# A two-layer attention trunk: gate paths ahead of the attention, values in six PSUM groups, an opening in units of 1, 2, 2, 2, 1 k-tiles

## The chip, the core and the metric

The kernel runs on one core of one Trainium2 chip. The metric is device time in microseconds (us) of one execution. The profiled execution is one of several; the trace belongs to it alone.

## What is computed

x has 256 tokens of 1024 features, c is one conditioning vector of 1024. There are two layers; each is a normalisation with shift and scale from c, an input projection, attention, a SiLU gate and an output projection. Everything is float32.

```python
for layer in range(DEPTH):
    ada = jnp.einsum('bd,de->be', c_act, w_ada[layer]) + b_ada[layer]
    shift, scale, gate = jnp.split(ada, 3, axis=-1)
    h = rms_norm(x, norm_g[layer]) * (1.0 + scale[:, None, :]) + shift[:, None, :]
    y = even_mixer(...) if layer % 2 == 0 else odd_mixer(...)
    x = x + gate[:, None, :] * y
return rms_norm(x, final_g)
```

The even mixer (layer 0) has two head groups. A: 8 heads of 64, one key and value head, window 128, a learned sink per head. B: 8 heads, 2 key and value heads, three branches (15 compressed blocks made by a small network, selected blocks, a window), added with sigmoid gates. The odd mixer (layer 1) has 16 heads of causal attention at this length. In both the attention's output is multiplied by silu(z), z a part of the input projection, and goes through the output projection.

## The kernel before

The program is not issued as it is written. `Plan.record` (L229) notes each instruction with what it depends on, and `Plan.issue` (L259) issues them all in the order of the table `ORDER` (L36 to L168). So the order on each engine is that of the table, and every instruction has line L256 in the profile; one goes by tiles. `plan.group` (L223) keeps matmuls together that use a part of TensorE's rows or columns at a time. For each tag a ring of buffers is taken in turn: five `raw` of 1 MB for weights that arrive (`RAW`), four `t4`, five `sm` and four `pT` for attention, and PSUM banks by tag (three pj, two s, one each of pt, o and m).

Every float32 product of a projection is three matmuls of halves: weights are cast to `whi` on ScalarE and the rest `wlo` is subtracted on VectorE (`split` L498), h likewise (hhi, hlo), and `mm3` (L533) adds hi x hi, hi x lo and lo x hi in PSUM.

**Opening.** c and x are read; x is transposed on TensorE into xT (part of bigA). The sums of squares of x give 1/rms, which is spread over the partitions by a matmul with `ones` and copied to `rb`. Then come eight k-tiles of 128 features. For each, 1 MB of w_ada (1024 rows, 128 columns each for shift and scale) arrives in runs of 512 bytes (`ada_tile` L401) and is summed with c as weights, by TensorE (`ada_rows` L419, 16 matmuls with 32-column weights in four column groups) or by VectorE (8 products of 256 columns into `acc`), as `ST_ON` says. `ada_shift_scale` (L450) makes the tile's shift and scale. `start_prep` (L688) then makes h from xT, rb, shift and scale with two products on VectorE and one activation, and loads the row of W_in: 128 features by 1688 columns, in four DMAs. `start_mm` (L712) adds the row's part for all 1688 columns, for two blocks of tokens, in PSUM: 24 matmuls. The w_ada of the next tile is loaded ahead of a tile's row, all in SP's queue.

**Layer 0.** After the opening come the remaining 256 columns of queries, rotation (`rope`), transposes, and the attention. `attn_pair` (L585) does one branch of two heads: four matmuls for the scores (a group), mask and minimum on VectorE, exponentials on ScalarE, four normalisations `sm<-sm,rc` on VectorE, six transposes, two copies, and four matmuls with the values into PSUM bank o (a group). B calls it twice a head pair (`b_pair` L938), A once (`a_pair` L924): 12 calls. `fin_o` (L790) copies the result to oT. The compressed branch is prepared by `compress` (L797) and `cmp_softmax` (L875); its keys `kcbd` and values `vz` are placed in blocks by two and eight small products onto memory that GpSimd had cleared. `cmp_pair` (L955) multiplies into a group of its own and adds it to oT on VectorE. `gated` (L970), four times, projects z (48 matmuls), takes tanh, and makes (1 + tanh) z and its product with oT on VectorE, then the two halves ghi and glo. Between these, `fill` places jobs: the sums with c for the gate of layer 0 and for shift and scale of layer 1. `out_proj` (L1025) follows.

**Layer 1** normalises and transposes x, then does four quads of heads (`attn_quad` L1115), each with its projections; after all of them come four `gated`, the output projection, the final norm and the output.

## Time and profile before

| | us |
|---|---|
| median of 3 runs | 318.71 |
| lowest, highest run | 318.41, 320.02 |
| the profiled execution's own time | 317.62 |
| its span in the trace | 315.8 |
| TensorE (PE) busy | 300.0 |
| VectorE (DVE) busy | 271.1 |
| ScalarE (ACT) busy | 189.9 |
| GpSimd (POOL) busy | 12.3 |

DMA moved 71.85 MB, 227 GB/s on the mean. How to read the lines: each group has the engine, the operation, out<-in with the program's tile names, the shapes, a count, then busy time, the mean ns of one and the idle time before them. A line of waits has the waiting engine and tile, the releaser, total us, count and longest. PEld is TensorE's weight load, which runs beside its matmuls. SP is the engine that issues most DMAs.

### The profile page before, as it was taken

How to read it: one execution, taken by the hardware profiler on the slowest of the kernel's cores; microseconds unless marked ns; L12 is line 12 of the kernel's file. 1: busy time of each engine (PE TensorE's matmuls, PEld its weight loads, DVE VectorE, ACT ScalarE, POOL GpSimd, SP SyncE). 2: the span in 40 equal slices, each digit the busy share in tenths (PEclk: the TensorE clock that was granted, in tenths of full speed). 3: DMA queues.
4: the chain of work that ended last, by engine and by line, in shares of the span. 5: the costliest groups of instructions: out<-in, count | busy, mean ns of one | idle time of the engine just before them, and what ended most of it. 6: DMA issues, size and time to landing. Idle time of an engine off the chain costs nothing.

```text
span 315.8 us, 6311 instructions
## 1 busy us (share of the span) xinstructions
PE 300.0 (95%) x2246; PEld 251.0 (79%) x2246; DVE 271.1 (86%) x744; ACT 189.9 (60%) x481; POOL 12.3 (4%) x30
## 2 busy tenths in 40 slices
PE   6788999999899999999999999999999999999991
PEld 6656787887677677898787689997899889988890
DVE  0289998999999999999998967787999998996873
ACT  3445435783758797797356675382965497654611
POOL 4200000000000000000010100000000000000021
PEclk9799999999999999999999999999999999999998
DMA  5999999999989954829699957646188644651003
GB/s 188 315 323 317 332 319 338 324 347 345 345 258 330 290 179 135 260 82 324 196 298 320 327 145 251 206 120 205 49 279 270 203 131 138 211 200 60 1 2 133
DMA packets 71280, 71.85 MB, mean 227 GB/s; under 512 B 3080, under 2 KB 62928, under 8 KB 71248
## 3 DMA queue, kind: packets, MB, share of 16 engines
q1 hardware_dynamic: 70528, 70.90, 72.0%
q10 hardware_dynamic: 592, 0.48, 0.5%
q8 instruction: 18, 0.29, 0.4%
q14 instruction: 14, 0.11, 0.1%
q0 software_dynamic: 128, 0.05, 0.1%
HBM read 70.38 MB, written 1.05 MB: 226 GB/s over the span
## 4 chain that ended last, share of the span: by engine, by line
PE 57%; DVE 22%; DMA 9%; ACT 4%; issue 4%; SPq 2%; POOL 1%; POOLq 0%; ACTq 0%; DVEq 0%
PE ps_pj L256 41%; DVE t L256 5%; DVE acc L256 5%; PE ps_pt L256 5%; PE ps_s L256 5%; PE ps_o L256 5%; DVE wlo L256 4%; DVE sm L256 4%; PE ps_m L256 2%; SPq L256 2%; DMA qT<-in_w_ada_dram 2%; DMA gate<-in_w_ada_dram 2%; DMA snk<-in_a_sinks_dram 2%; DMA raw<-in_w_in_even_dram 2%; DMA raw<-in_w_in_odd_dram 2%
## 5 line engine op out<-in xcount | busy, mean ns | idle before, releaser
L256 ACT CAST whi<-raw 128x512 fp32r<-128x512 f32 (+1 forms) x132 | 76.4, 600 | 47.4 <-PE ps_pj L256 28.9
L256 DVE TENSOR_TENSOR wlo<-raw,whi 128x512 fp32r<-128x512 f32 (+1 forms) x116 | 74.4, 659 | 5.4 <-ACT whi L256 5.3
L256 PE MATMUL ps_pj<-hhi,whi 128*128 128x256 f32 x256 | 73.0, 289 | 0.0
L256 PE MATMUL ps_pj<-hhi,wlo 128*128 128x256 f32 x256 | 72.2, 285 | 0.0
L256 PE MATMUL ps_pj<-hlo,whi 128*128 128x256 f32 x256 | 72.0, 283 | 0.0
L256 PEld LDWEIGHTS ps_pj<-hhi,whi 128*128 128x128 f32 x256 | 47.9, 188 | 1.4 <-issue 0.8
L256 PEld LDWEIGHTS ps_pj<-hlo,whi 128*128 128x128 f32 x256 | 48.1, 188 | 0.7 <-issue 0.3
L256 PEld LDWEIGHTS ps_pj<-hhi,wlo 128*128 128x128 f32 x256 | 47.9, 188 | 0.5 <-issue 0.2
L256 ACT ACTIVATE sm<-sm,mn 128x128 f32<-128x128 f32 (+1 forms) x76 | 34.1, 450 | 12.0 <-DVE mn L256 11.9
L256 DVE SCALAR_TENSOR_TENSOR acc<-raw,cz,acc 128x512 f32<-128x512 f32 x42 | 31.4, 746 | 0.5
L256 PE MATMUL ps_pj<-wlo,hhi 128*128 128x512 f32 (+2 forms) x72 | 27.3, 379 | 0.0
L256 PE MATMUL ps_pj<-whi,hhi 128*128 128x512 f32 (+2 forms) x72 | 26.3, 381 | 0.8 <-ACT hhi L256 0.7
L256 PE MATMUL ps_pj<-whi,glo 128*128 128x512 f32 (+1 forms) x72 | 26.7, 371 | 0.0
L256 PE MATMUL ps_pj<-wlo,ghi 128*128 128x512 f32 (+1 forms) x72 | 26.7, 371 | 0.0
L256 PE MATMUL ps_pj<-whi,ghi 128*128 128x512 f32 (+1 forms) x72 | 26.6, 374 | 0.0
L256 PE MATMUL ps_pj<-whi,hlo 128*128 128x512 f32 (+2 forms) x72 | 26.4, 368 | 0.0
L256 DVE SCALAR_TENSOR_TENSOR wlo<-raw,whi 128x512 fp32r<-128x512 f32 x32 | 21.0, 688 | 3.7 <-ACT whi L256 3.4
L256 DVE TENSOR_SCALAR sm<-sm,rc 128x256 f32<-128x256 f32 (+1 forms) x76 | 21.8, 318 | 0.3
L256 ACT COPY pT<-ps_pt 128x384 f32<-128x384 f32 x33 | 15.5, 471 | 10.2 <-PE ps_pt L256 9.5
L256 PE MATMUL ps_pt<-ta,sm 128*128 128x128 f32 x114 | 20.4, 280 | 0.0
L256 PEld LDWEIGHTS ps_pt<-ta,sm 128*128 128x128 f32 x114 | 13.0, 141 | 4.8 <-issue 2.9
L256 PEld LDWEIGHTS ps_pj<-whi,hhi 128*128 128x128 f32 x72 | 13.3, 188 | 3.6 <-ACT hhi L256 1.4
(206 smaller groups left out, 566.3 us busy)
## 6 DMA issues: line engine op xcount, KB each, us to landing
raw<-in_w_in_odd_dram SPq DMA_DIRECT2D x16, 1024.0 KB, 5.7
raw<-in_w_ada_dram SPq DMA_DIRECT2D x28, 512.0 KB, 5.6
qT<-in_w_ada_dram SPq DMA_DIRECT2D x24, 256.0 KB, 5.8
raw<-in_w_in_even_dram SPq DMA_DIRECT2D x5, 1024.0 KB, 7.2
raw<-in_w_in_even_dram SPq DMA_DIRECT2D x8, 576.0 KB, 5.5
raw<-in_w_out_even_dram SPq DMA_DIRECT2D x4, 1024.0 KB, 5.1
raw<-in_w_out_odd_dram SPq DMA_DIRECT2D x4, 1024.0 KB, 5.4
gate<-in_w_ada_dram SPq DMA_DIRECT2D x8, 256.0 KB, 6.1
```

The costliest lines, as they stand in the source:

```text
L256: self.ops.append(dict(key=eng.key, deps=deps, fn=lambda: getattr(real, name)(*args, **kw)))
```

## The change

Six things change together, and a new `ORDER` table puts them in another order.

1. *Opening.* `START` holds five units of 1, 2, 2, 2 and 1 k-tiles. A pair's w_ada is loaded at once, in runs of 1 KB (`start_ada`), into the rooms of qT and gate or into the four t4 in turn. The second number says how many of the eight row blocks VectorE sums (in 512 columns for a pair); TensorE takes the rest and adds VectorE's partial sums by a matmul with `ones` (`start_sums`), and a transpose puts the sums on the partitions. A row of W_in comes in two DMAs, with columns 256 to 640 in place of 0 to 256 and 512 to 640. x is multiplied by 1/rms ahead of its transposes, so hhi comes from xT in one activation.
2. *Gates first.* `gate_path` projects z and leaves (1 + tanh) z in oT. `gated` multiplies it by the attention's result straight from PSUM; `gated_parts` makes the halves. `fin_o`'s copies in layer 0 are gone. In layer 1 the gate path stands inside each quad.
3. *Values in six groups.* `attn_four` does two branches or two head pairs and returns the transposed weights; `attn_values` then multiplies all with the values, in one group and one PSUM bank. A has two groups of eight matmuls, B four of ten, with the compressed branch's two in front.
4. *Normalisation.* `ON_ACT` gives two of an `attn_four`'s eight normalisations, both of 256 columns, to ScalarE.
5. *Masks.* `blk` holds 0.5 in blocks and zero elsewhere: one product places the compressed keys, one the values.
6. *Order.* A goes first, then the compressed branch, then B.

The first place is SP's queue in the opening: names on the left are the rooms, w_ada and w_in_even the sources. Before:

```order
L256 DMA raw_101<-in_w_in_even_dram 128x152
L256 DMA qT_95<-in_w_ada_dram 128x4x128 x2
L256 DMA qT_96<-in_w_ada_dram 128x4x128 x2
L256 DMA raw_102<-in_w_in_even_dram 128x256
L256 DMA raw_102<-in_w_in_even_dram 128x1152
L256 DMA raw_102<-in_w_in_even_dram 128x128
L256 DMA raw_102<-in_w_in_even_dram 128x152
L256 DMA qT_97<-in_w_ada_dram 128x4x128 x2
L256 DMA gate<-in_w_ada_dram 128x4x128 x2
L256 DMA raw_103<-in_w_in_even_dram 128x256
```

And after, from the end of row 0 to row 3:

```order
L258 DMA raw_100<-in_w_in_even_dram 128x384
L258 DMA t_86<-in_w_ada_dram 128x2x256 x2
L258 DMA t_87<-in_w_ada_dram 128x2x256 x2
L258 DMA t_88<-in_w_ada_dram 128x2x256 x2
L258 DMA t_89<-in_w_ada_dram 128x2x256 x2
L258 DMA raw_101<-in_w_in_even_dram 128x1304
L258 DMA raw_101<-in_w_in_even_dram 128x384
L258 DMA qT_97<-in_w_ada_dram 128x2x256 x2
L258 DMA qT_98<-in_w_ada_dram 128x2x256 x2
L258 DMA qT_99<-in_w_ada_dram 128x2x256 x2
L258 DMA gate<-in_w_ada_dram 128x2x256 x2
L258 DMA raw_102<-in_w_in_even_dram 128x1304
```

One k-tile of w_ada (a pair of lines of x2) stood between rows before; now two k-tiles stand ahead of rows 1, 2 and 4, one ahead of row 6, and none between rows 2 and 3.

The second place is TensorE in B's head pairs; ps_o is the bank of the results, vb the values, pT the transposed weights, pcT and vz the compressed branch. Before:

```order
L256 MATMUL ps_o_93<-pT_140,vb 64x256
L256 MATMUL ps_o_93<-pT_141,vb 64x256
L256 MATMUL ps_o_93<-pT_140,vb 64x128
L256 MATMUL ps_o_93<-pT_141,vb 64x128
L256 MATMUL ps_pt_81<-ta,sm_132 128x128 x3
L256 MATMUL ps_pj_86<-hhi,whi_109 128x256
L256 MATMUL ps_pj_86<-hlo,whi_109 128x256
L256 MATMUL ps_pj_86<-hhi,wlo_113 128x256
```

And after, one whole group:

```order
L258 MATMUL ps_o_96<-pcT,vz 64x256 x2
L258 MATMUL ps_o_96<-pT_130,vb 64x256
L258 MATMUL ps_o_96<-pT_131,vb 64x256
L258 MATMUL ps_o_96<-pT_130,vb 64x128
L258 MATMUL ps_o_96<-pT_131,vb 64x128
L258 MATMUL ps_o_96<-bigA,vb 64x256 x2
L258 MATMUL ps_o_96<-bigA,vb 64x128 x2
```

The two branches and the compressed one, three groups with other work between them before, stand together.

```diff
-ST_ON = "ppvvpvvp"
-AHEAD = 1
+START = ((1, 0), (2, 4), (2, 6), (2, 6), (1, 4))
+GROUPED = 1
...
+ON_ACT = ((0, 1, 1), (1, 1, 1))
...
-            uses.append((a.tensor.name + "#", (p0, p1, 1), eng.key == "pe" and not accum))
+            uses.append((a.tensor.name + "#", (p0, p1, 1), eng.key == "pe" and (not accum or bool(kw.get("stop")))))
...
+                    if (n, i, t) in ON_ACT:
+                        A.mul(sms[i][:, a:b], sms[i][:, a:b], rc[:, n, i, t : t + 1])
+                    else:
+                        V.tensor_scalar(sms[i][:, a:b], sms[i][:, a:b], rc[:, n, i, t : t + 1], None, op0=ALU.mult)
...
+    def attn_values(po, jobs):
         ids = []
-        for t, (a, b) in enumerate(((0, P), (P, 3 * P))):
-            for i in range(2):
-                q, kT = qk[i]
-                ids.append(T.matmul(pSs[i][:, a:b], q(t), kT[:, 0 : b - a], start=True, stop=True))
+        for n, (cs, keys) in enumerate(jobs):
+            for m, (os, heads) in enumerate(keys):
+                for i in range(2):
+                    ids.append(T.matmul(
+                        po[64 * i : 64 * i + 64, cs + os.start : cs + os.stop],
+                        heads[i][0],
+                        heads[i][1],
+                        start=n == 0 and m == 0,
+                        stop=n == len(jobs) - 1 and m == len(keys) - 1,
+                        skip_group_check=True,
+                        tile_position=(0, 64 * i),
...
+        r = r0[:, t, :]
+        A.activation(t4(), xs[:, t, :], AF.Square, scale=D**-0.5, accum_out=r[:, 0:1])
+        G.tensor_scalar(r[:, 0:1], r[:, 0:1], EPS, None, op0=ALU.add)
+        G.tensor_tensor(r[:, 1:2], r[:, 0:1], ex0[:, 0:1], ALU.pow)
+        xn = t4()
+        V.tensor_scalar(xn[:, :512], xs[:, t, :512], r[:, 1:2], None, op0=ALU.mult)
+        A.mul(xn[:, 512:], xs[:, t, 512:], r[:, 1:2])
+        for hh in range(2):
+            px = bank("s" if t == 0 else "pj")
+            for j in range(4):
+                T.transpose(px[:, j * P : (j + 1) * P], xn[:, (4 * hh + j) * P : (4 * hh + j + 1) * P], ident)
+            (V.tensor_copy if hh == 0 else A.copy)(xT[:, 4 * hh : 4 * hh + 4, t * P : (t + 1) * P], px.rearrange("p (j s) -> p j s", j=4))
...
-        if ST_ON[g] == "v":
-            a = acc0[:, (g % 2) * 256 : (g % 2) * 256 + 256]
-            V.tensor_scalar(a, w[0][:, 0, :], cz[:, 0, 0:1], None, op0=ALU.mult)
-            for k in range(1, KT):
-                V.scalar_tensor_tensor(a, w[k // 4][:, k % 4, :], cz[:, k, 0:1], a, op0=ALU.mult, op1=ALU.add)
-            ada_shift_scale(0, g, 1, a=a, st=ones)
-        else:
-            ada_shift_scale(0, g, 1, a=ada_rows(w))
...
+        kk = 4 // n
+        w = []
+        for i in range(2 * n):
+            wt = room[i].rearrange("p (k s c) -> p k s c", k=kk, s=2)
+            for s in range(2):
+                Y.dma_start(wt[:, :, s, :], src[:, kk * i : kk * i + kk, s, P * g : P * (g + n)])
+            w += [wt[:, k] for k in range(kk)]
...
+    def start_sums(g, n, d, w):
+        a = sb([P, 512], "acc", 1)
+        av = a[:, : 256 * n].rearrange("p (s c) -> p s c", s=2)
+        for k in range(d):
+            if k == 0:
+                V.tensor_scalar(av, w[k], cz[:, k, 0:1], None, op0=ALU.mult)
+            else:
+                V.scalar_tensor_tensor(av, w[k], cz[:, k, 0:1], av, op0=ALU.mult, op1=ALU.add)
...
+            tq = [(cz[:, k, :], w[k][:, s_, cs]) for k in ks if k >= d]
+            if d and 0 in ks:
+                tq.append((ones[:, 0:32], av[:, s_, cs]))
...
+        T.transpose(pc[:, :P], asb[:, :P], ident)
...
-        Y.dma_start(raw[:, 1432:1688], W0[g * P : (g + 1) * P, 0:256])
-        Y.dma_start(raw[:, 0:1152], W0[g * P : (g + 1) * P, 1152:2304])
-        Y.dma_start(raw[:, 1152:1280], W0[g * P : (g + 1) * P, 512:640])
-        Y.dma_start(raw[:, 1280:1432], W0[g * P : (g + 1) * P, 2304:2456])
+        Y.dma_start(raw[:, 0:1304], W0[g * P : (g + 1) * P, 1152:2456])
+        Y.dma_start(raw[:, 1304:1688], W0[g * P : (g + 1) * P, 256:640])
+        return raw
+    def start_prep(g, raw):
         h = oT[:, 3 + g % 2, :]
-        V.scalar_tensor_tensor(h, xT[:, g, :], shs[:, 0, 1, g : g + 1], rb, op0=ALU.mult, op1=ALU.mult)
-        A.activation(hhi[:, g, :], h, AF.Identity, bias=shs[:, 0, 0, g : g + 1])
-        V.scalar_tensor_tensor(hlo[:, g, :], h, shs[:, 0, 0, g : g + 1], hhi[:, g, :].bitcast(F32), op0=ALU.add, op1=ALU.subtract)
+        sc, sh = shs[:, 0, 1, g : g + 1], shs[:, 0, 0, g : g + 1]
+        A.activation(hhi[:, g, :], xT[:, g, :], AF.Identity, bias=sh, scale=sc)
+        V.tensor_scalar(h, xT[:, g, :], sc, sh, op0=ALU.mult, op1=ALU.add)
+        V.tensor_tensor(hlo[:, g, :], h, hhi[:, g, :].bitcast(F32), ALU.subtract)
...
+    rooms = [spare[0:2], more, spare, more, spare[0:2]]
+    ahead, g = start_ada(0, START[0][0], rooms[0]), 0
+    for u, (n, d) in enumerate(START):
+        w, rows_w = ahead, [start_row(g)]
+        if u + 1 < len(START):
+            ahead = start_ada(g + n, START[u + 1][0], rooms[u + 1])
+        rows_w += [start_row(g + v) for v in range(1, n)]
+        start_sums(g, n, d, w)
+        preps = [start_prep(g + v, rows_w[v]) for v in range(n)]
+        for v in range(n):
+            start_mm(g + v, *preps[v])
+        g += n
...
-            V.tensor_scalar(kcbd[rs, :, 16 * i : 16 * i + 16], pk[rs, 0:32].rearrange("p (g b) -> p g b", g=2), 0.5, None, op0=ALU.mult)
+        V.tensor_tensor(
+            kcbd.rearrange("p g (i b) -> p g i b", i=2),
+            pk[:, 0:32].rearrange("p (g b) -> p g b", g=2).unsqueeze(2).to_broadcast([P, 2, 2, 16]),
+            blk[:, 4:6].unsqueeze(1).unsqueeze(3).to_broadcast([P, 2, 2, 16]),
...
-                V.tensor_scalar(vz[rs, g, j, :], pv[rs, 0:HD], 0.5, None, op0=ALU.mult)
+                T.matmul(pv[:, HD * g : HD * g + HD], hr[:, j, :, :].rearrange("p a b -> p (a b)"), w2["v"][:, j, :], start=(j == 0), stop=(j == 1))
+        V.tensor_tensor(
+            vz,
+            pv[:, : 2 * HD].rearrange("p (g d) -> p g d", g=2).unsqueeze(2).to_broadcast([P, 2, 4, HD]),
+            blk[:, 0:4].unsqueeze(1).unsqueeze(3).to_broadcast([P, 2, 4, HD]),
...
+        gated(po, 2 * u, 2, 0.5)
+        gated_parts(2 * u)
...
+        pts = attn_four([keys(0), keys(1)], maskc, None, [gv[:, 2 * hp_ : 2 * hp_ + 2, :, 1 + br] for br in range(2)])
         po = bank("o")
-        for br in range(2):
-            qk, vcl = [], []
-            for i in range(2):
-                rs = slice(64 * i, 64 * i + 64)
-                qk.append(
-                    (
-                        (lambda t, rs=rs: qbT[rs, hp_, t * P : (t + 1) * P]),
-                        kTb[rs, 2 * br + g, :],
-                    )
-                )
-                vcl.append(lambda b: vb[:, b, 3 * br + g, :])
-            attn_pair(qk, maskc, vcl, None, gv[:, 2 * hp_ : 2 * hp_ + 2, :, 1 + br], po, br == 0, br == 1)
-        fin_o(po, 4 + hp_)
-    def cmp_pair(hp_):
-        g = hp_ // 2
-        po = bank("o")
-        for i in range(2):
-            T.matmul(
-                po[64 * i : 64 * i + 64, :S],
-                vz[:, g, (2 * hp_ + i) % 4, :],
-                pcT[:, g, :],
-                start=True,
-                stop=True,
-                tile_position=(0, 64 * i),
-            )
-        V.tensor_tensor(oT[:, 4 + hp_, :], oT[:, 4 + hp_, :], po[:, :S], ALU.add)
-    def gated(w, zc, ft, coef, tag="pj"):
+        attn_values(po, ([(0, cmp_keys(hp_))] if cmp else []) + [(0, keys_of(lambda b, br=br: vb[:, b, 3 * br + g, :], pts[br])) for br in range(2)])
+        gated(po, 4 + hp_, 1, 0.25)
+        if hp_ % 2:
+            gated_parts(3 + hp_)
...
-        V.tensor_tensor(oT[:, 4 + hp_, :], oT[:, 4 + hp_, :], po[:, :S], ALU.add)
...
+    def gate_path(w, zc, ft, tag="pj"):
         pz = proj_F(w, zc, tag)
-        tt = t4()
-        th, og = tt[:, :512], tt[:, 512:].rearrange("p (j s) -> p j s", j=2)
+        th = oT[:, ft : ft + 2, :].rearrange("p j s -> p (j s)")
         A.activation(th, pz, AF.Tanh, scale=0.5)
         V.scalar_tensor_tensor(th, th, 1.0, pz, op0=ALU.add, op1=ALU.mult)
-        V.scalar_tensor_tensor(
-            og.rearrange("p j s -> p (j s)"),
-            oT[:, ft : ft + 2, :].rearrange("p j s -> p (j s)"),
-            coef,
-            th,
-            op0=ALU.mult,
-            op1=ALU.mult,
-        )
-        A.copy(ghi[:, ft : ft + 2, :], og)
-        V.tensor_tensor(glo[:, ft : ft + 2, :], og, ghi[:, ft : ft + 2, :].bitcast(F32), ALU.subtract)
+    def gated(po, ft, n, coef):
+        V.scalar_tensor_tensor(oT[:, ft : ft + n, :], po[:, : n * S].rearrange("p (a s) -> p a s", s=S), coef, oT[:, ft : ft + n, :], op0=ALU.mult, op1=ALU.mult)
+    def gated_parts(ft):
+        A.copy(ghi[:, ft : ft + 2, :], oT[:, ft : ft + 2, :])
+        V.tensor_tensor(glo[:, ft : ft + 2, :], oT[:, ft : ft + 2, :], ghi[:, ft : ft + 2, :].bitcast(F32), ALU.subtract)
...
-        A.copy(oT[:, 2 * u : 2 * u + 2, :], po.rearrange("p (a s) -> p a s", a=2))
+        gated(po, 2 * u, 2, 0.5)
+        gated_parts(2 * u)
+    jobs += ada_jobs(ada_gate, 1, G1_ON, 2)
...
+        gate_path(W1, 3 * D + 256 * u, 2 * u, "p1")
         attn_quad(u, qk)
```

More of the change, by code (lines that the diff above doesn't have):

```diff
@@ L342, in tile_trunk @@
     G.memset(ex0, -0.5)
+    blk = const([P, 6], "blk")
+    G.memset(blk, 0.0)
+    for j in range(6):
+        rs = slice(32 * j, 32 * j + 32) if j < 4 else slice(64 * j - 256, 64 * j - 192)
+        G.memset(blk[rs, j : j + 1], 0.5)
     cz = const([P, KT, 32], "cz")
@@ L647, in tile_trunk, with keys_of @@
+    def keys_of(vcols, pts):
+        return [
+            (os, [(vcols(b), pts[i][:, ks]) for i in range(2)])
+            for b, (ks, os) in enumerate(((slice(0, S), slice(0, S)), (slice(S, 3 * P), slice(P, S))))
+        ]
     bigA = const([P, 2304], "bigA")
@@ new lines, in tile_trunk, with a_quad, keys @@
+    pj_banks, s_banks = ring["ps_pj"][0], ring["ps_s"][0]
+    ring["ps_pj"] = [pj_banks[0:3], 0]
+    m_banks = ring["ps_m"][0]
+    ring["ps_s"] = [s_banks + pj_banks[3:3], 0]
+    def a_quad(u):
+        def keys(i):
+            rs = slice(64 * i, 64 * i + 64)
+            return lambda n, t: (qaT[rs, 2 * u + n, t * P : (t + 1) * P], kTb[rs, 4, : P * (t + 1)])
+        sk = [[[snk[:, o + 4 * u + 2 * n + i : o + 4 * u + 2 * n + i + 1] for i in range(2)] for n in range(2)] for o in (8, 0)]
+        pts = attn_four([keys(0), keys(1)], maska, sk, None)
+        po = bank("o")
+        attn_values(po, [(n * S, keys_of(lambda b: vb[:, b, 2, :], pts[n])) for n in range(2)])
+        gated(po, 2 * u, 2, 0.5)
+        gated_parts(2 * u)
```

325 lines of the change are left out of this document (159 added, 166 removed), and 262 rows, old and new, of the table ORDER.

## The prediction

> **What bounds the kernel now.** I read the page's first two parts, then a table of stages, then the waits of the weight loads between 62 and 180 us, the chain between 108 and 135 us and the costliest groups of VectorE.
>
> The page gives the span, the busy shares, and the slices of 7.9 us.
>
> ```profile
> span 315.8 us, 6311 instructions
> PE 300.0 (95%) x2246; PEld 251.0 (79%) x2246; DVE 271.1 (86%) x744; ACT 189.9 (60%) x481; POOL 12.3 (4%) x30
> ...
> PE   6788999999899999999999999999999999999991
> ...
> DVE  0289998999999999999998967787999998996873
> ```
>
> The stage table has the stretch, then busy time of PE, PEld, DVE, ACT and POOL, the granted clock, the DMA share and GB/s.
>
> ```profile
> 0.00:18.00 18.00, 13.04 (x87) 10.82 (x88) 3.24 (x14) 8.56 (x18) 5.09 (x18) 0.91 0.91 259
> 18.00:62.00 44.00, 42.20 (x235) 32.93 (x236) 40.17 (x96) 20.73 (x47) 0.00 (x0) 1.00 1.09 325
> 62.00:112.00 50.00, 48.13 (x430) 37.13 (x429) 49.30 (x187) 35.41 (x110) 1.58 (x3) 1.00 1.00 321
> 112.00:150.00 38.00, 37.95 (x315) 31.36 (x314) 37.62 (x123) 31.24 (x95) 0.00 (x0) 1.00 0.57 191
> 180.00:250.00 70.00, 70.00 (x563) 64.84 (x566) 59.57 (x142) 42.84 (x99) 0.00 (x0) 1.00 0.63 196
> 260.00:303.00 43.00, 43.00 (x291) 37.44 (x290) 36.81 (x67) 25.87 (x52) 0.90 (x2) 1.00 0.35 115
> ```
>
> Three regimes stand there. Until 62 us the DMA engines are full (share 1.09, 325 GB/s). In layer 0's attention, 62 to 150 us, TensorE and VectorE are both nearly full: VectorE is busy 49.30 + 37.62 = 86.92 of 88 us. In layer 1 TensorE alone is full, and VectorE has about 15% free. But a busy PE is not a PE at its peak: its weight loads still wait for semaphores in the middle stage.
>
> ```profile
> PEld ps_m L256 <- DVE vz L256: 1.1, 2, 0.7
> PEld ps_pt L256 <- ACT sm L256: 1.0, 2, 0.6
> ...
> PEld ps_m L256 <- DVE h L256: 0.2, 1, 0.2
> ```
>
> These are the first two and the last of 21 rows (total us, count, longest) that name another engine; together they hold 10.2 us. So at most some 10 us of layer 0 can be won by relieving other engines, and the rest only by giving TensorE less to do.
>
> **Part 1, the opening (0 to 62 us).** The last row's cast waits for its load until 55.84, and the opening's last matmul starts at 63.47, the next work at 63.66.
>
> ```profile
> 11.96 0.27 PE L256 MATMUL ps_pt<-ta,crow 8*128 8x8 f32 x1
> ...
> 12.95 1.07 PE L256 MATMUL ps_m<-qT,cz 128*32 128x256 f32 x16
> ...
> 17.88 0.74 PE L256 MATMUL ps_pj<-whi,hhi 128*128 128x512 f32 x2
> ...
> 55.84 0.62 ACT L256 CAST whi<-raw 128x512 fp32r<-128x512 f32 x1 [0.34 <-DMA raw<-in_w_in_even_dram]
> ...
> 63.47 0.35 PE L256 MATMUL ps_o<-whi,hlo 128*128 128x408 f32 x1
> 63.66 0.60 PE L256 MATMUL ps_pt<-ta,bigA 128*128 128x128 f32 x4
> ```
>
> The first main matmul (17.88) should come earlier: c is no longer transposed behind x (11.96), and the broadcast of 1/rms is gone. I put it at 15.2, a guess on which nothing hangs: any start up to 17.5 gives the same end, since row 1 lands when it did. Bytes in queue order: x 1.05 MB, w_ada 1.05 MB per k-tile, a row of W_in 0.86 MB. Before, the queue holds x, two k-tiles of w_ada, row 0, one k-tile and row 1: 5.92 MB. After, it holds x, one k-tile, row 0, a pair and row 1: the same 5.92 MB. By 18 us 259 x 18 = 4.66 MB had moved; with the rate of 20 to 30 us (329 GB/s, quoted below) row 1 lands at 18 + 1.26/0.329 = 21.8, and with 1.2 us for its cast and subtraction, twice the cast's 0.62, tile 1 starts at 23.0. Row 2 is different: a whole pair stands before it, so 8.88 MB are needed against 7.83 before, and it lands at 30.8, 3.2 us later than before. Tile 2 starts at 32.0. A tile takes (45.8 - 1.8)/8 = 5.5 us (17.88 to 63.66, less TensorE's idle 44 - 42.20), so TensorE waits 32.0 - 28.5 = 3.5 us there. Row 4 also stands one k-tile further back, at 12.70 MB: it is ready at 43.6, where tile 4 would be due at 43.0. Four tiles from there end at 65.6: **+1.9 us**. The other rows have the byte counts that they had.
>
> Bounds: for the better, the end is held by the bytes, 1.05 for x, 8 x 1.05 of w_ada and 8 x 0.86 of rows, some 16.35 MB altogether.
>
> ```profile
> 20.00:30.00 10.00, 9.72 (x46) 7.54 (x47) 9.64 (x25) 3.11 (x7) 0.00 (x0) 1.00 1.11 329
> ...
> 70.00:80.00 10.00, 9.86 (x106) 7.65 (x109) 9.70 (x43) 4.32 (x16) 1.58 (x3) 1.00 1.09 343
> ```
>
> The first stretch moves w_ada in runs of 512 bytes beside the rows, the second has only longer ones: 329 against 343 GB/s. After the change pairs come in 1 KB runs; at the second rate the bytes take 47.7 us instead of 49.7, a gain of 2.0 as the bound. The Trainium skill ("DMA: Bandwidth & Descriptors", Specifications) puts the line-rate limit at 512 bytes or more; by that rule the longer runs bring nothing, this bound would be 0 instead of -2.0, and the sum would stand. The trace agrees nearly: the difference is 4%. For the worse, the pair's tiles t4 are also the room in which x is squared and scaled, so SP's queue waits there with rows 1 to 7 behind it; another 3.5 us, the size of the wait before tile 2, gives +5.4. VectorE's share in the opening falls (16 products with shift and scale at 0.48 become 16 simpler ones; sums in 512 columns):
>
> ```profile
> L256 DVE SCALAR_TENSOR_TENSOR acc<-qT,cz,acc 128x256 f32<-128x256 f32 x20 | 9.7, 484 | 0.6
> ...
> L256 DVE SCALAR_TENSOR_TENSOR hlo<-oT,shs,hhi 128x256 fp32r<-128x256 f32 x7 | 3.4, 482 | 0.1
> ```
>
> This is worth a few us on VectorE, but bytes lead there, so I take 0.
>
> **Part 2, layer 0's attention and gates.** What VectorE does there:
>
> ```profile
> L256 DVE TENSOR_SCALAR sm<-sm,rc 128x256 f32<-128x256 f32 x24 | 8.4, 360 | 0.1
> L256 DVE SCALAR_TENSOR_TENSOR t<-oT,t 128x512 f32<-128x512 f32 x4 | 2.7, 686 | 0.1
> L256 DVE SCALAR_TENSOR_TENSOR t<-t,ps_pj 128x512 f32<-128x512 f32 x4 | 2.7, 682 | 0.1
> L256 DVE TENSOR_SCALAR vz<-ps_m 32x64 f32<-32x64 f32 x8 | 1.8, 220 | 0.1
> L256 DVE TENSOR_TENSOR oT<-oT,ps_o 128x256 f32<-128x256 f32 x4 | 1.7, 414 | 0.0
> ...
> L256 DVE TENSOR_TENSOR gate<-ps_m,gate 128x512 f32<-128x512 f32 x1 | 0.7, 684 | 0.0
> ```
>
> - Twelve of the 24 normalisations go to ScalarE: -12 x 0.360 = -4.3.
> - Four additions of the compressed branch go, since it shares the PSUM group: -4 x 0.414 = -1.7.
> - Eight small products for the compressed values become one of 512 columns: -8 x 0.220 + 0.684 = -1.1; two for the keys become one: -0.2.
> - The product with the gate reads PSUM, four times 128x512 (4 x 0.686 = 2.7) before, then twice 128x512 and four times 128x256 (2 x 0.682 + 4 x 0.484 = 3.3): +0.6.
>
> Sum on VectorE: -6.7 us out of a stage where 1.1 us is free. The products out of PSUM are a place where a rule speaks against the change. One-input products show it in the trace:
>
> ```profile
> L256 DVE TENSOR_SCALAR t<-ps_s,shs 128x128 f32<-128x128 f32 x8 | 3.0, 403 | 0.0
> ...
> L256 DVE TENSOR_SCALAR sm<-sm,rc 128x128 f32<-128x128 f32 x24 | 6.6, 281 | 0.0
> ```
>
> From PSUM 403 ns, from SBUF 281. The two-input products that `gated` uses cost the same either way (682 with PSUM, 686 without), so I charge nothing. The Trainium skill ("VectorE: DVE Perf Modes", Why PSUM operands drop a tier) says that a PSUM operand holds fp32 at the slowest rate; by that rule, read for every product and with the row's 0.122 us for each 128 columns, two products of 512 columns and four of 256 would cost 16 x 0.122 = 2.0 more, and the sum would be that much higher. The trace agrees for one input, not for two.
>
> TensorE sheds group changes. The chain names the groups (each fp32 matmul is recorded as two passes):
>
> ```profile
> 115.43 1.45 PE ps_o L256 x16
> ...
> 124.37 0.58 PE ps_o L256 x4
> ...
> 130.31 0.80 PE ps_o L256 x8
> ```
>
> Before: eight groups for B's two branches and four for A at 0.80, and four compressed ones at 0.58: 12 x 0.80 + 4 x 0.58 = 11.9. After: two groups of eight matmuls (x16) at 1.45, four of ten at 1.45 + 0.58, less 0.15 for the change that is saved (2 x 0.80 - 1.45): 2.9 + 7.5 = 10.4. So -1.5 on TensorE.
>
> ScalarE takes the twelve normalisations and loses the copies out of PSUM:
>
> ```profile
> L256 ACT COPY oT<-ps_o 128x256 f32<-128x256 f32 x9 | 3.3, 370 | 1.2 <-PE ps_o L256 1.0
> ...
> L256 ACT ACTIVATE t<-t 128x256 f32<-128x256 f32 x1 | 0.4, 417 | 0.3 <-DVE t L256 0.3
> ```
>
> 12 x 0.417 - 8 x 0.370 = +2.0, in a stage where it has 88 - 66.65 = 21 us free; if that cover fails, 2.0 is the price. The bounds for the stage: TensorE's -1.5 alone, if nothing else waits less, to -1.5 less most of the 10.2 us of waits: -10. I take **-5.5**, nearer VectorE's 6.7, because it is the fuller engine; the 1.2 us between are what I leave to waits that the new order brings.
>
> A new wait: values start only when all branches of a head pair are done and, for B, when the compressed branch is there. On PE the projections of the gates are queued round it, and they cover it.
>
> **Part 3, layer 1 and the tail.** Gates move between the quads and four copies go from ScalarE. TensorE is busy 70.00 of 70.00 and 43.00 of 43.00 us with the same matmuls: **0**, from -1.5 (the group changes' size again) to +1.5.
>
> The profiled execution's own time is 317.62 (its span of 315.8 and 1.8 around it). The sum against it: 317.6 + 1.9 - 5.5 = 314.0. It is 1.1 us below the median of the three runs, 318.71, so the median comes out at **315.1**.
>
> **The rivals.**
> - *Both gains come whole* (faster). Row 2's wait is hidden by work already loaded, the longer runs bring 2.0, and layer 0 loses 9: 317.6 - 2.0 - 9 + 1.1 = 307.7. For it: VectorE is full for 88 us. Against: TensorE's idle in 112:150 is only 0.05. Chance 0.17.
> - *TensorE becomes the bound at once* (no change). VectorE's 6.7 is slack nobody needs; only -1.5 stays and the opening eats it: 317.6 + 1.9 - 1.5 + 1.1 = 319.1. For it: PE busy 48.13 of 50 and 37.95 of 38. Against: the 10.2 us of waits. It is also what would be seen if the regrouping did not do what it says. Chance 0.15.
> - *Paired loads starve TensorE* (slower). SP holds at the t4 rooms and rows 2 and 4 stand behind one k-tile more: +5.4, with only -1.5 behind it: 317.6 + 5.4 - 1.5 + 1.1 = 322.6. It decides from the point where the opening's last matmul lies later than 63.7 + 5.5, about 69. For it: 325 GB/s is all the queue gives. Against: only two of eight rows stand later in the order of bytes. Chance 0.13.
>
> **How the numbers follow.** The forecast keeps 0.55, with a range of its own of 311.5 to 318.5. A measurement of this kernel can tell about 0.5%, 1.6 us: faster is below 317.1, slower above 320.3. Faster: most of 0.55, say 0.49, and 0.17, together 0.66. Same: 0.15 and 0.06 of the forecast, 0.21. Slower: 0.13. The range of 8 in 10 reaches to the price of the fast rival and short of that of the slow one: 307.5 to 321.5.
>
> **What would show it.** Tile 1's first main matmul near 23, tile 2's after a wait for row 2 near 32, before tile 4 hardly one, the last of the opening near 65.6; VectorE's busy time in the attention stage some 6.7 lower; fewer waits of PEld; layer 1 as long as before. The forecast is wrong if the opening's end moves by over 3 us, if layer 0's attention is shorter by under 3 or over 8 us, or if layer 1's length changes by over 2.

## The result and the profile after

The changed kernel takes 307.85 us (median of 4 runs, 306.97 to 309.57), the one before 319.26 (4 runs): a ratio of 0.965, 95% interval 0.9595 to 0.9704. The forecast was 315.1 with a range of 307.5 to 321.5 and a gain of 1.1%; the gain is 3.5%, three times that.

The page of the changed kernel, its span, its busy shares, and the slices, which are 7.6 us long now:

```profile
span 304.9 us, 6320 instructions
PE 290.6 (95%) x2292; PEld 247.9 (81%) x2292; DVE 262.8 (86%) x709; ACT 189.6 (62%) x484; POOL 12.0 (4%) x35
...
PE   7688999999999999999999999999999999999991
...
DVE  0679988899999999999989968998779898996973
```

The same stretches as in the prediction's table of stages:

```profile
0.00:18.00 18.00, 13.70 (x94) 11.36 (x94) 7.81 (x24) 9.01 (x17) 5.09 (x23) 1.00 0.91 308
18.00:62.00 44.00, 41.77 (x306) 34.23 (x306) 38.32 (x82) 25.64 (x65) 0.00 (x0) 1.00 1.07 370
62.00:112.00 50.00, 49.56 (x467) 41.61 (x466) 49.58 (x187) 40.21 (x126) 1.54 (x3) 1.00 0.85 273
112.00:150.00 38.00, 38.00 (x298) 30.33 (x296) 37.42 (x113) 27.49 (x76) 0.00 (x0) 1.00 0.79 247
```

The line to stop at is the second. The DMA engines are as full as before (1.07 against 1.09), yet they move 370 GB/s in place of 325. In the attention TensorE's idle time is down to 0.4 us, and VectorE is as full as it was (49.58 + 37.42 of 88).

Three places in TensorE's timeline cut the span into stages that both kernels have: the start of the first main matmul, of the opening's last one into ps_s, and of the last one of layer 0's output projection. The changed kernel:

```profile
14.18 0.73 PE L258 MATMUL ps_pj<-whi,hhi 128*128 128x512 f32 x2 [1.55 <-ACT hhi L258]
...
60.56 0.40 PE L258 MATMUL ps_s<-whi,hlo 128*128 128x512 f32 x1
...
162.76 0.40 PE L258 MATMUL ps_s<-whi,glo 128*128 128x512 f32 x1
```

And the kernel before, with 17.88 quoted in the prediction. The opening's work into ps_s runs on behind the row at 63.47 that the prediction took for its last:

```profile
65.02 0.39 PE L256 MATMUL ps_s<-whi,hlo 128*128 128x512 f32 x1
...
172.67 0.40 PE L256 MATMUL ps_pj<-whi,glo 128*128 128x512 f32 x1
```

| stage, us | before | after | change | forecast |
|---|---|---|---|---|
| to the first main matmul | 17.9 | 14.2 | -3.7 | -2.7 |
| opening, first to last | 47.1 | 46.4 | -0.8 | +4.6 |
| the two together | 65.0 | 60.6 | -4.5 | +1.9 |
| layer 0 after it | 107.6 | 102.2 | -5.4 | -5.5 |
| layer 1 and tail | 143.1 | 142.1 | -1.0 | 0 |

Layer 0 is right to 0.1 us. What failed is the opening, by 6.4 us. There ScalarE's casts wait for the rows as follows:

```profile
20.62 0.62 ACT L258 CAST whi<-raw 128x512 fp32r<-128x512 f32 x1 [0.18 <-DMA raw<-in_w_in_even_dram]
...
28.83 1.14 ACT L258 CAST whi<-raw 128x512 fp32r<-128x512 f32 x2 [5.23 <-DMA raw<-in_w_in_even_dram]
...
39.11 1.66 ACT L258 CAST whi<-raw 128x512 fp32r<-128x512 f32 x3 [5.21 <-DMA raw<-in_w_in_even_dram]
```

These are rows 1, 2 and 4. The prediction had them land at 21.8, 30.8 and 42.4 (the last is its 43.6 less the 1.2 us for cast and subtraction): each cast starts earlier than that, row 4's by 3.3 us.

The second trace of the changed kernel, taken later on another occasion, starts its main matmuls at 15.85 and ends the opening at 63.06, 2.0 us earlier than before in place of 4.5; its layer 0 is 102.3 long. So the opening's gain differs between executions, and the stages of one trace are read beside the medians. Eight traces below leave the changed opening as it is (these two and six whose edits lie in layer 0): they start it at 13.9 to 15.9 and end it at 60.5 to 63.1, which is 2.0 to 4.6 us before 65.02. The kernel before moves as well: a version of it that is the same up to its third k-tile (b_lean below) starts at 18.9.

### The profile page after: what moved, and what is told of

Read it like the earlier page. It is cut to its first block, busy times and chain, and to the rows that moved or that the text cites. A ratio compares the mean times of both kernels' runs of the same rounds, so it can differ in the third digit from the quotient of the medians.

```text
span 304.9 us, 6320 instructions
## 1 busy us (share of the span) xinstructions
PE 290.6 (95%) x2292; PEld 247.9 (81%) x2292; DVE 262.8 (86%) x709; ACT 189.6 (62%) x484; POOL 12.0 (4%) x35
## 3 DMA queue, kind: packets, MB, share of 16 engines
HBM read 70.38 MB, written 1.05 MB: 234 GB/s over the span
## 4 chain that ended last, share of the span: by engine, by line
PE 85%; DMA 5%; DVE 3%; POOL 2%; issue 2%; ACT 1%; POOLq 0%; ACTq 0%; DVEq 0%; SPq 0%
PE ps_pj L258 53%; PE ps_s L258 11%; PE ps_pt L258 8%; PE ps_o L258 7%; PE ps_m L258 6%; DMA qT<-in_w_ada_dram 2%; DMA t<-in_w_ada_dram 2%; DVE acc L258 1%; DMA ta<-in_tbl_a_dram 1%; DVE t L258 1%; POOL parts L258 1%; POOL r L258 1%; ACT t L258 1%; DVE xs L258 0%; DVE wlo L258 0%
## 5 line engine op out<-in xcount | busy, mean ns | idle before, releaser
L258 PE MATMUL ps_pj<-hhi,whi 128*128 128x256 f32 x256 | 72.2, 287 | 0.0
L258 PE MATMUL ps_pj<-hhi,wlo 128*128 128x256 f32 x256 | 71.0, 285 | 0.0
L258 ACT ACTIVATE sm<-sm,mn 128x128 f32<-128x128 f32 (+1 forms) x58 | 26.0, 450 | 13.1 <-DVE mn L258 13.1
L258 PE MATMUL ps_pj<-whi,ghi 128*128 128x512 f32 (+1 forms) x56 | 20.6, 369 | 0.0
L258 PE MATMUL ps_pj<-whi,glo 128*128 128x512 f32 (+1 forms) x56 | 20.5, 366 | 0.0
L258 PE MATMUL ps_pj<-wlo,ghi 128*128 128x512 f32 (+1 forms) x56 | 20.5, 369 | 0.0
L258 PE MATMUL ps_pt<-ta,sm 128*128 128x128 f32 x87 | 16.9, 279 | 0.0
L258 ACT COPY pT<-ps_pt 128x384 f32<-128x384 f32 x25 | 11.9, 474 | 6.4 <-PE ps_pt L258 6.2
L258 PEld LDWEIGHTS ps_pj<-whi,hlo 128*128 128x128 f32 x72 | 13.6, 189 | 1.9 <-issue 0.2
L258 PEld LDWEIGHTS ps_pj<-wlo,hhi 128*128 128x128 f32 x72 | 13.5, 188 | 1.9 <-DVE wlo L258 0.2
```

What stands on the lines that cost most here:

```text
L258: self.ops.append(dict(key=eng.key, deps=deps, fn=lambda: getattr(real, name)(*args, **kw)))
```

## The experiments

Theory R says that the opening gained by the longer runs of its loads. Theory S says that it gained by its earlier start. For layer 0, theory V has VectorE as the limit and theory P has TensorE with its changes between groups. All times are medians; the ratio is to the kernel before on the same chip, and a difference such as +1.9 us is to 307.85. The changed kernel itself, measured again on another chip, took 309.28 (ratio 0.9663). So a difference of under some 2 us between medians tells little by itself, and the length of the stage in the trace is given with it: layer 0 takes 102.2 to 102.7 us in six traces whose edits, if any, lie in the opening; with more work on VectorE there (a_vopen) it takes 103.3.

**Runs of 512 bytes.** The paired k-tiles' w_ada in runs of 512 bytes again, same bytes, same count of loads:

```diff
-                Y.dma_start(wt[:, :, s, :], src[:, kk * i : kk * i + kk, s, P * g : P * (g + n)])
...
+                else:
+                    m = 2 * i + s
+                    k4, sv, v = 4 * (m // 4), (m % 4) // 2, m % 2
+                    Y.dma_start(
+                        wt[:, s].rearrange("p s c -> p (s c)").rearrange("p (q c) -> p q c", q=4),
+                        src[:, k4 : k4 + 4, sv, P * (g + v) : P * (g + v + 1)],
+                    )
```

This version also lets an instruction be issued behind its place in `ORDER` where its inputs come later; in the trace the opening's loads are issued in the same order and number as in the changed kernel.

> The changed kernel, with the w_ada of the paired k-tiles read again in runs of 512 bytes, by as many loads of the same size (each load takes four row blocks of 128 columns; they land in other places of the tiles, so shift and scale of six k-tiles are computed from the wrong numbers). Theory R, the run length: the opening gained because longer runs move w_ada faster (370 GB/s between 18 and 62 us against 325 before). 6.3 MB at 325 in place of some 400 GB/s take 3 to 6 us longer, ahead of rows 1 to 7, so the total rises by 3 to 6 us, to 311 to 314, and the rate of 18 to 62 us falls to 335 or less. Theory S, the earlier start: the opening gained because its first main matmul came 3.7 us earlier and the steps of a tile got shorter, and the rate is a symptom; the total stays within 1 us of 307.9.

Measured: 312.25, ratio 0.9806 (0.9753 to 0.9859), 4.4 us above 307.85. The table of stages, for 18 to 62 us:

```profile
18.00:62.00 44.00, 39.64 (x275) 32.53 (x276) 33.41 (x73) 21.02 (x53) 0.00 (x0) 0.92 1.05 338
```

The DMA share is still 1.05, but the rate is down to 338 GB/s. The opening starts at 14.06 and ends at 65.33: 51.3 us long. The casts of rows 2 and 4 start at 32.2 and 43.6, 3.3 and 4.4 us later than in the changed kernel, and the opening ends 4.8 us later. The granted clock of this stretch is 0.92 where the changed kernel has 1.00, so a little of the cost can be the clock's; the rows' lateness covers most of it. Theory R holds, S falls for this edit.

**Four loads for each row.**

```diff
-        Y.dma_start(raw[:, 0:1304], W0[g * P : (g + 1) * P, 1152:2456])
-        Y.dma_start(raw[:, 1304:1688], W0[g * P : (g + 1) * P, 256:640])
...
+            plan.sync.real.dma_start(raw[:, 0:1152], wr[:, 1152:2304]),
+            plan.sync.real.dma_start(raw[:, 1152:1304], wr[:, 2304:2456]),
...
+            plan.sync.real.dma_start(raw[:, 1304:1560], wr[:, 256:512]),
+            plan.sync.real.dma_start(raw[:, 1560:1688], wr[:, 512:640]),
```

> The changed kernel, with each row of W_in loaded by four DMAs again (1152, 152, 256 and 128 columns) in place of two (1304 and 384). Theory R: short runs of 512 and 608 bytes come back for a quarter of each row and SP issues 16 more loads; at most 2.5 us of DMA time over eight rows, so +1 to +2 us. Theory S: within 0.5 us.

Measured: 309.77, ratio 0.9712 (0.9681 to 0.9743), +1.9 us. In its trace the opening is 47.4 us long and starts at 16.1, where the second trace of the unchanged version starts at 15.85 and takes 47.2. So the traces show the edit worth 0.2 to 1 us in length, and the medians can't tell more. Inconclusive by itself. The rate between 18 and 62 us falls to 345 GB/s here too, nearly as far as with 512-byte runs, but the cast of row 2 starts at 29.6 as in the second trace and that of row 4 at 40.8 against 39.2. What counts is when the rows come, and the mean rate of the stretch is only a sign of it.

**Both.**

> Both edits together: 512-byte runs for w_ada and four loads for each row (shift and scale of six k-tiles are computed from the wrong numbers). Theory R: the bytes move as before the change, the opening's gain of 4.7 us is gone or turns into the loss of 1.9 that the prediction had, since row 2 stands behind a pair: +4.7 to +6.6, total 312.5 to 314.5. Theory S: within 1 us of 307.9.

Measured: 314.02, ratio 0.9861 (0.9823 to 0.9899), +6.2 us. Two stretches of the opening:

```profile
18.00:30.00 12.00, 9.16 (x66) 7.19 (x66) 8.13 (x17) 3.13 (x7) 0.00 (x0) 0.72 0.99 303
30.00:46.00 16.00, 13.18 (x105) 10.08 (x105) 10.63 (x23) 5.73 (x13) 0.00 (x0) 1.00 0.99 313
```

ScalarE's waits between 18 and 62 us:

```profile
ACT whi L258 <- DMA raw<-in_w_in_even_dram: 19.7, 5, 7.7
```

And the opening's last matmul:

```profile
67.92 0.40 PE L258 MATMUL ps_s<-whi,hlo 128*128 128x512 f32 x1
```

At 303 and 313 GB/s the casts wait 19.7 us for rows, 7.7 at most, TensorE is idle for 2.8 of each of these stretches, and the opening ends at 67.92, 2.9 us later than in the kernel before although it starts some 4 us earlier. So the opening gets longer as the prediction said (+2.9 where it had +1.9), and the total is 1.1 us from its forecast. That closeness is partly luck: the casts of rows 2 and 4 start at 32.3 and 45.2, later than its 30.8 and 42.4, while TensorE starts 1.3 us before its guess.

**A late start.** Idle matmuls ahead of the first k-tile's transpose:

```diff
...
+                [plan.tensor.real.matmul(pc[:, :P], ones, ones, start=True, stop=True) for _ in range(LATE)],
```

> The changed kernel, with 18 idle matmuls of 128 columns with ones ahead of the transpose of the first k-tile's sums, some 3.9 us on TensorE, so that the first main matmul starts near 18 as before the change. Theory R: the rows' landing leads, so most of the delay disappears in the waits for rows 1 and 2: +0 to +1.5 us. Theory S: the start is what was gained: +3 to +3.9 us.

Measured: 311.18, ratio 0.9769 (0.9733 to 0.9805), +3.3 us. The first main matmul starts at 17.83 and the opening is 46.0 us long, so the delay of 3.65 us (14.18 to 17.83) is passed on but for 0.4. Against the second trace, which starts at 15.85 at a lower clock (last section), the opening ends only 0.7 us later, so what a start is worth depends on that too. Theory S holds for this edit, and R, which expected the rows to swallow it, falls. Both are true of the changed kernel: with rows that land early enough, the opening's end follows its start; with short runs it follows the rows.

**The kernel before with longer runs alone.**

```diff
-                    Y.dma_start(w[:, :, s * P : (s + 1) * P], src[:, ks, cols[s] * P : (cols[s] + 1) * P])
+                    k2 = slice(4 * u + 2 * s, 4 * u + 2 * s + 2)
+                    Y.dma_start(w[:, 2 * s : 2 * s + 2, :], src[:, k2, cols[0] * P : (cols[0] + 2) * P])
```

> The kernel before, with the opening's w_ada loads in runs of 1 KB: each load takes two row blocks of 256 adjacent columns in place of four row blocks of 128 (same bytes and count; layer 0's scale is computed from the wrong columns). Theory R for the opening: the rate of 18 to 46 us rises from 324 to some 370 GB/s and its waits for rows go, -1.5 to -2.5 us, since TensorE still starts at 17.9 and loses its waits alone (it was idle 1.8 us between 18 and 62 and waited in part beside that). Theory S: no change, within 0.7 us.

Measured: 319.57 against 319.30, ratio 1.0003 (0.9976 to 1.003): nothing. ScalarE's waits in 18 to 62 us of the kernel before:

```profile
ACT whi L256 <- DMA raw<-in_w_in_even_dram: 13.8, 10, 2.8
ACT hhi L256 <- DVE oT L256: 4.8, 3, 2.3
ACT hhi L256 <- DVE shs L256: 3.1, 2, 1.6
```

and with longer runs:

```profile
ACT hhi L256 <- DVE oT L256: 8.4, 4, 3.2
ACT hhi L256 <- DVE shs L256: 5.6, 3, 2.8
ACT whi L256 <- DMA raw<-in_w_in_even_dram: 3.4, 3, 1.3
```

The wait for rows falls from 13.8 to 3.4 us, and the wait for VectorE's sums and products rises from 7.9 to 14.0. The opening is as long as before, 47.1 us (from 19.0 to 66.14). A wait took the place of the one removed.

**Less VectorE in the kernel before, alone and with the runs.** Every second sum of w_ada on one column:

```diff
+                if k % 2:
+                    plan.ops[-1]["fn"] = lambda k=k, a=a: plan.vector.real.scalar_tensor_tensor(a[:, 0:1], w[k // 4][:, k % 4, 0:1], cz[:, k, 0:1], a[:, 0:1], op0=ALU.mult, op1=ALU.add)
```

> The kernel before, with 16 of the 28 sums that VectorE adds up in the opening cut to one column (so shift and scale of four k-tiles are wrong): some 16 x 0.42 = 6.8 us of VectorE's time less. Theory W, the opening of before stands against two limits of about the same height, the landing of the rows and VectorE's work for each tile: with the rows as they were, under -1 us. Theory S, only the start of the first main matmul matters: no change, within 0.7 us. Theory D, VectorE alone was the limit: -2.5 to -4.7 us.

Measured: 318.95, ratio 0.9995 (0.9963 to 1.0027): nothing again, and the opening takes 47.1 us (18.9 to 66.05). VectorE is busy for 4.0 us less between 18 and 62 us, but ScalarE's wait for the rows stays:

```profile
ACT whi L256 <- DMA raw<-in_w_in_even_dram: 13.3, 10, 2.4
```

With both edits:

> The kernel before with both: VectorE's sums cut as above, and w_ada in runs of 1 KB, which alone had changed nothing (shift and scale are computed from the wrong numbers). Theory W: both limits fall together, -2 to -4.7 us. Theory S: within 0.7 us. Theory D: the same as with the cut alone.

Measured: 317.36, ratio 0.9927 (0.9899 to 0.9955): -1.8 us by the medians, -2.3 by the ratio, at the lower end of what theory W expected. The opening is 44.8 us long in place of 47.1:

```profile
18.08 0.73 PE L256 MATMUL ps_pj<-whi,hhi 128*128 128x512 f32 x2
...
62.88 0.40 PE L256 MATMUL ps_s<-whi,hlo 128*128 128x512 f32 x1
```

ScalarE's waits now:

```profile
ACT hhi L256 <- DVE oT L256: 6.5, 4, 2.5
ACT whi L256 <- DMA raw<-in_w_in_even_dram: 4.2, 3, 1.6
ACT hhi L256 <- DVE shs L256: 4.1, 2, 2.1
```

Two limits of nearly the same height, and only both edits together lower it: theory W. In this trace layer 0 behind the opening takes 109.2 us in place of 107.6, so part of the gain is lost again there; why was not tried.

**More VectorE in the changed opening.**

```diff
...
+        plan.ops[-1]["fn"] = lambda: [e_(), plan.vector.real.tensor_scalar(h, h, 1.0, None, op0=ALU.mult)]
```

> The changed kernel with one idle product by 1 of 128x256 on VectorE in each k-tile's preparation, 8 x 0.36 = 2.9 us of VectorE's time in the opening and on the way to hlo. Theory W: VectorE still is near its limit there, +1 to +2.9 us. If TensorE alone sets the opening's pace now: under +0.7 us.

Measured: 308.86, ratio 0.9671 (0.9634 to 0.9708), +1.0 us, and the intervals overlap. Its trace has the opening 48.5 us long against 46.0 to 47.4 in the eight traces without such an edit. VectorE seems still near its limit there, but the times don't settle it.

**Normalisations back on VectorE.**

```diff
-ON_ACT = ((0, 1, 1), (1, 1, 1))
+ON_ACT = ()
```

> The changed kernel with all normalisations on VectorE again (ON_ACT empty): twelve of 128x256 move back, 12 x 0.36 = 4.3 us of VectorE's time in layer 0's attention. Theory V, VectorE sets the pace of that stage: its 5.2 us gain shrinks in that proportion, +2.5 to +4.3 us on the total (310.5 to 312). Theory P, TensorE sets it and gained by fewer group changes: under +0.7.

Measured: 309.88, ratio 0.9702 (0.966 to 0.9745), +2.0 us; layer 0 takes 104.9 in the trace in place of 102.2. By the median this lies between the theories, nearer to V; the stage's +2.7 is within what V expected.

**VectorE's whole saving back.**

```diff
+        plan.ops[-1]["fn"] = lambda: [plan.vector.real.tensor_scalar(o_, o_, 1.0, None, op0=ALU.mult), g_()][-1]
...
+        plan.ops[-1]["fn"] = lambda: [z_()] + [plan.vector.real.tensor_scalar(v_, v_, 1.0, None, op0=ALU.mult) for _ in range(6)]
```

> As before (ON_ACT empty), and beside it idle VectorE work for what the shared group and the masks saved: a 128x256 product by 1 on oT ahead of each of the four products with the gate of B, and six 32x64 products by 1 on the placed values. That is some 4.3 + 4 x 0.36 + 6 x 0.2 = 7 us of VectorE more than in the changed kernel. Theory V: +5 to +7 us. Theory P: under +1.5.

Measured: 313.79, ratio 0.9809 (0.977 to 0.9847), +5.9 us; layer 0 takes 107.4 us, against 107.6 before the change. The weight loads wait most for this, which in the changed kernel stood at 0.3 us:

```profile
PEld ps_s L258 <- DVE mn L258: 2.2, 5, 0.9
```

Scores wait until VectorE has read the bank ahead of them. Theory V holds: the work given back, 6.4 us by its rows' durations (4.2 + 1.1 + 1.1) where 7 were expected, is worth 5.2 of the stage.

VectorE's busy time over the whole stage (the third busy time of a line, behind PE and PEld) shows it more closely. In this order the kernel before, the changed kernel, the run with the normalisations back and the run with the whole saving back:

```profile
65.42:173.07 107.65, 105.73 (x848) 83.51 (x850) 105.53 (x348) 74.47 (x217) 3.10 (x6) 1.00 0.83 263
60.96:163.16 102.20, 101.32 (x845) 82.52 (x846) 99.77 (x328) 75.66 (x219) 2.92 (x6) 1.00 0.84 265
61.69:166.55 104.86, 102.78 (x844) 83.02 (x846) 102.46 (x340) 71.70 (x207) 2.92 (x6) 1.00 0.82 258
61.12:168.49 107.37, 103.66 (x845) 82.94 (x846) 104.61 (x350) 71.81 (x207) 2.93 (x6) 1.00 0.80 253
```

VectorE's busy time and the stage's length go up and down together: +2.7 and +2.7 with the normalisations, +4.8 and +5.2 with the whole, and the change itself took 5.8 and 5.4. Twelve normalisations of 0.35 us add 2.7 us and not 4.2: a VectorE instruction can begin before the one ahead of it has ended (in the changed kernel one begins at 92.46 and lasts 0.75 us, the next begins at 93.12), so its duration is more than what it costs.

**Values in 16 groups.** The code places each branch's group among the projections ahead of the joint one:

```diff
-        plan.group(ids)
+            plan.group(ids)
+            if n < len(jobs) - 1:
+                plan.early.append((ids, 0.3 if len(jobs) == 3 and n == 0 else 0.6))
```

> The changed kernel with the values' matmuls as 16 groups in place of six: each branch's four, the compressed branch's two and each of A's head pairs stand apart, among projections, in the same bank and with no more work on any engine. Theory V: under +0.5 us. Theory P: ten changes more between forms of matmul at 0.15 to 0.3 us each: +1.5 to +3 us.

Measured: 314.85, ratio 0.985 (0.9811 to 0.9889), +7.0 us; layer 0 takes 109.4. That is over twice what theory P expected, on no more work. Two causes were possible, the changes of group or the earlier place, and the next run tells them apart.

**14 groups, each shortly ahead of the joint one's place.**

```diff
-                plan.early.append((ids, 0.3 if len(jobs) == 3 and n == 0 else 0.6))
+                plan.early.append((ids, 0.9 if len(jobs) == 3 and n == 0 else 1.0))
```

> The changed kernel with 14 groups of values in place of six, each of the eight more standing shortly ahead of where its joint group stood, with a few projections or transposes between, so that the PSUM bank isn't taken early and no matmul waits earlier than before. Theory C, a change of group costs TensorE a fixed time (the run with 16 groups: 7.0 / 10 = 0.7 us each): +5 to +6 us. Theory E, most of the 7.0 came from standing early, by waits for the scores and the bank: +1.5 to +3 us, 0.2 to 0.35 us for each change.

Measured: 313.48, ratio 0.9819 (0.9795 to 0.9844), +5.6 us on the medians and 5.1 by the ratios; layer 0 takes 106.8, +4.6. (B's first head pair keeps its joint group, hence 14.) So eight more changes cost 0.6 us each, near theory C. One place shows what is in it. In the changed kernel all that uses a part of TensorE stands in one piece, the sums of w_ada (ps_m), the scores (ps_s), the values of A's second group (ps_o) and scores again:

```profile
104.53 1.07 PE L258 MATMUL ps_m<-raw,cz 128*32 128x256 f32 x16
105.53 0.93 PE L258 MATMUL ps_s<-kTb,qT 64*128 64x128 f32 x8
106.39 0.87 PE L258 MATMUL ps_o<-bigA,vb 128*64 128x256 f32 x8
107.09 0.82 PE L258 MATMUL ps_o<-pT,vb 128*64 128x256 f32 x8
107.84 0.93 PE L258 MATMUL ps_s<-kTb,qT 64*128 64x128 f32 x8
```

With 14 groups the first four of these values (two passes each in the record) stand ahead, and the second scores come to a bank that VectorE hasn't read:

```profile
107.07 0.87 PE L260 MATMUL ps_o<-bigA,vb 128*64 128x256 f32 x8
108.13 1.07 PE L260 MATMUL ps_m<-raw,cz 128*32 128x256 f32 x16
109.13 0.93 PE L260 MATMUL ps_s<-kTb,qT 64*128 64x128 f32 x8
109.99 0.87 PE L260 MATMUL ps_o<-pT,vb 128*64 128x256 f32 x8
111.43 0.93 PE L260 MATMUL ps_s<-kTb,qT 64*128 64x128 f32 x8 [0.57 <-DVE mn L260]
```

Four matmuls with the values now stand between two groups of scores where eight stood, and the second scores wait 0.57 us for VectorE: they start 2.30 us after the first ones, as before (2.31). In the stage TensorE is idle for 2.3 us in place of 0.9, so idle time is 1.5 of the 4.6 us. How much of the rest is the change of form and how much hidden waits, no run here separates.

**Both edits of layer 0** (VectorE's whole saving back, and 16 groups) **and the changed kernel again.**

> The changed kernel with both edits of layer 0 together: VectorE's 7 us of work back (alone +5.9) and the values in 16 groups (alone +7.0). Each alone costs more than the 5.2 us that layer 0 gained. Theory X, two limits side by side, VectorE and TensorE's order of the groups, of which the later one counts: +7 to +8.5 us. Theory Y, the costs add up, since TensorE waits for VectorE at one place and VectorE for TensorE at another: +11 to +13 us, and then the rest of the change gave layer 0 nothing or took from it.

> The changed kernel as it is, on the same chip as the run with both edits, so that small differences of the runs with one more product in each k-tile and with three normalisations on ScalarE can be told: 307 to 309 us.

Measured, on one chip: 318.69 (ratio 0.9952, 0.9921 to 0.9983) and 309.28 (ratio 0.9663, 0.9622 to 0.9705): +9.4 us, and layer 0 takes 112.3 in place of 102.3. That lies between the theories, above X's 8.5 and below Y's 11. The stage's +9.9 is nearer to the sum of the two (5.2 + 7.2 = 12.4) than to the larger, so the costs add up for the most part. They come to more than the 5.4 that layer 0 gained. It may be that the split groups stand in an order that wasn't made for them; the new order by itself was not tried.

**Three normalisations of eight on ScalarE.**

```diff
-ON_ACT = ((0, 1, 1), (1, 1, 1))
+ON_ACT = ((0, 1, 1), (1, 0, 1), (1, 1, 1))
```

> The changed kernel with three of eight normalisations on ScalarE in place of two (six more of 128x256, 2.2 us of VectorE's time, 2.5 us of ScalarE's). From the step before (twelve moved back cost 2.0 us, 0.16 us each): if VectorE still sets the pace, -0.5 to -1.5 us; if ScalarE or TensorE does, 0 to +1 us.

Measured: 309.66, ratio 0.9691 (0.9643 to 0.9739): not faster, and layer 0 takes 103.2 in place of 102.2 or 102.3. ScalarE's normalisation takes longer than the row that the prediction used, as the changed kernel's own row shows:

```profile
L258 ACT ACTIVATE sm<-sm,rc 128x256 f32<-128x256 f32 x9 | 4.5, 504 | 1.6 <-DVE rc L258 1.6
```

504 ns in place of 417, and 360 on VectorE in the kernel before. Whether this is why, no run shows. No version of these beats the changed kernel.

## Why the prediction was wrong

**The step that failed** is the opening's rate, and with it two sentences: "with the rate of 20 to 30 us (329 GB/s, quoted below) row 1 lands at 18 + 1.26/0.329" and "any start up to 17.5 gives the same end, since row 1 lands when it did". The sum took both its bytes by 18 us (4.66 MB) and its rate behind that from the kernel before. The changed kernel has moved 308 x 18 = 5.5 MB by 18 us, and then:

```profile
18.00:30.00 12.00, 9.77 (x98) 6.87 (x97) 9.85 (x19) 4.40 (x10) 0.00 (x0) 1.00 1.06 382
30.00:46.00 16.00, 16.00 (x105) 13.50 (x104) 14.77 (x34) 8.90 (x20) 0.00 (x0) 1.00 1.07 368
```

With these numbers the same sum puts rows 1, 2 and 4 at 19.0, 26.7 and 37.0. Their casts start at 20.6, 28.8 and 39.1. So the sum also leaves out some 2 us between the count of bytes and the cast, which hid part of the other error; what these 2 us are was not tried. TensorE still waits, 2.2 us between 18 and 30 us, but no longer from 30 to 46, where the run with both loads as before waits another 2.8. So the earlier start counts: delayed by 3.65 us, it moved the end by 3.2.

The bound of -2.0 that the prediction gave for longer runs took a stretch with 343 GB/s, 70 to 80 us, as the ceiling. It was none: the mean packet there has 0.96 KB (3.43 MB in 3576 packets), and between 18 and 62 us it has 0.82 KB before the change and 1.22 KB after it, since the opening's rows come in runs of up to 5.2 KB beside w_ada's. The rule of the Trainium skill weighed there ("DMA: Bandwidth & Descriptors", Specifications, line rate from 512 bytes up) would have made the gain of the longer runs 0. The runs decide against it: with the same bytes and the same number of loads, 512 bytes in place of 1 KB for six of eight k-tiles take the rate from 370 to 338 GB/s and cost 4.4 us.

The prediction named its own sign of being wrong, an end of the opening that moves by over 3 us; it moved by 4.5 in the first trace and by 2.0 in the second.

**VectorE in the opening** was charged at nothing, "but bytes lead there". Shown wrong for the kernel before by the two edits that changed nothing alone and 2.3 us (by the ratio) together: bytes and VectorE led side by side.

**The start** was guessed at 15.2 and measured at 14.18 and 15.85.

**Layer 0** was -5.5 and is -5.4 (-5.3 in the second trace). VectorE's term is shown: its work back, 6.4 us by durations and 4.8 by busy time, takes 5.2. Its busy time over the stage fell by 5.8, where the prediction summed 6.7 from durations. The weight loads' waits for other engines between 62 and 180 us fell from 10.2 to 5.5 us, 13 rows left. The term of TensorE, -1.5 from 0.15 for each change of group, was too small: eight more changes cost 4.6. The two terms as measured come to more than 5.4 together, so that the sum was right to 0.1 us is partly luck: one term was too large, one too small, and they overlap.

**Gated from PSUM** was charged at nothing, against the rule of the Trainium skill that the prediction weighed for every product ("VectorE: DVE Perf Modes", Why PSUM operands drop a tier). The rows of the changed kernel, 256 and 512 columns:

```profile
L258 DVE SCALAR_TENSOR_TENSOR oT<-ps_o,oT 128x256 f32<-128x256 f32 x4 | 1.7, 422 | 0.0
L258 DVE SCALAR_TENSOR_TENSOR oT<-ps_o,oT 128x512 f32<-128x512 f32 x2 | 1.4, 686 | 0.0
```

686 ns out of PSUM as with both inputs in SBUF before: right.

**Layer 1 and the tail** were 0 and are -1.0, inside the bounds; no run tried why.

**The rivals.** "Both gains come whole" gave 307.7, close to the result, but with -2.0 in the opening and -9 in layer 0, so its closeness is luck. "TensorE becomes the bound at once" falls by the run that gives VectorE its work back. "Paired loads starve TensorE" goes the way of the run with both loads as before, at 314.0: that needs the shorter runs, and even there the opening ends at 67.92, short of the 69 at which this rival was to decide.
